# Reusing split weights at the start of the second token half, and data-paced constant matmuls, in a hybrid conv block

## Chip, cores and metric

The kernel runs on one core of a Trainium2 chip. The metric is the device time of one execution in microseconds, the median over runs. The profile is one separate execution, with its own time and span; all positions below are microseconds from the start of that span.

## The reference

One layer of a streaming encoder on 1024 tokens of 1024 channels (float32):

```python
h = rms_norm(x, norm_mix_g) * (1 + sc1) + sh1          # sh1, sc1, g1, ... = silu(c) @ w_ada + b_ada
proj = h @ w_in                                        # 1024 -> 7 x 1024
b_s, c_s, v_s, v_c, gl_c, gate_br = split(proj)
y_a = (b_s * causal_dwconv(c_s * v_s, conv_short_w)) @ w_short_out
u = v_c * sigmoid(gl_c)
u = causal_dwconv(u, conv_conf_w) + conv_conf_b        # width 31
y_b = silu(layer_norm(u)) @ w_conf_out
g_a, g_b = split(sigmoid(gate_br))
x = x + g1 * ((g_a * y_a + g_b * y_b) @ w_o)
h2 = rms_norm(x, norm_ffn_g) * (1 + sc2) + sh2
a, b = split(h2 @ w_ffn_in)
x = x + g2 * ((silu(a) * b) @ w_ffn_out)
out = rms_norm(x, final_norm_g)
```

## The kernel before

Activations lie transposed: 128 channels on the partitions, tokens along the row. [...] A matrix of weights comes in eight row chunks (128 input channels each) or column chunks.

For precision each float32 operand is split into a high part and a remainder: `split_w` (L208) has ScalarE (ACT) cast the loaded chunk `raw` to `wh` (L214) and VectorE (DVE) or GpSimd (POOL) subtract it to get `wl` (L215). The pools for `wh` and `wl` hold three chunks each, those for `raw` five in all. `mm3` (L301) then makes three matmuls per product: wh x high (L309), wh x remainder (L310), wl x high (L312). The first three chunks of the first stage, `WHOLE`, are multiplied unsplit in float32 (L305).

A list `plan` holds the order in which weights are loaded and split. `next_w(ahead)` takes the next ready chunk and first has `fetch` prepare `ahead` more; `AHEAD` is 2. The SP queue issues the loads in the order in which buffers come free. Each engine works its instructions in an order fixed when the program is built; a scheduler that models times chooses it, within the data dependencies and explicit `issue_after` hints.

The stages that the change touches:

- **Beginning** (L479 to L507). `c` is broadcast over the partitions by two matmuls into `cb` (L497). ACT squares the eight 512-token chunks of x into `sq` tiles (six-buffer pool `gs`), DVE adds them (`squares_x`, L428), two matmuls with a matrix of ones sum over channels into `ss` (`norm_start`, L440). ACT takes the reciprocal root into `rx0r` (L359) and squares it (L372); DVE refines it, writing `rx0r` in place (`rstd_negative`, L377 and L378); `modulate` scales x (DVE L388, ACT L392). `keep_clock` (L471) puts constant 128 x 128 matmuls of ones between: 7 before `cb`, 16 between `cb` and `ss`, 18 after `ss` (`CLOCK`).
- **Lead** (L554 to L560). Seven column blocks of the input projection by `row_blocks` (L408): for each row chunk k, all seven blocks, each in a PSUM bank of its own; then the same for the second half, with its own norm (`rx1`). `row_blocks` interleaves the last `joined` chunks block by block, so that banks finish one after the other. For the second half all eight chunks are loaded and split again (`again_w`).
- **yb** (L851 to L866). The Conformer branch's projection by `row_blocks` with eight blocks (all eight banks), first for one half, then the other. After a half each bank is multiplied with a gate tile `gb` on DVE (L860), which frees it; `join` adds `ma` (L848) and splits the sum into `mg` (ACT L340, DVE L341). The gate tiles come by DMAs that POOL issues (L859), six buffers for all. During the stage `next_b` also loads rows of `ada` into `raw` buffers, and DVE makes modulation values of them (L290).
- **Mix** (L872 to L887, L938 to L945). The output projection w_o, one column chunk after the other, first half then second half.

In yb and mix the plan loads all eight chunks of `w_conf` and `w_o` for each half. Every half takes the chunks in the order 0 to 7.

Of the kernel before, what the change touches and what calls it, by code (L numbers as in the profile page):

```python
# [65 lines left out]
WHOLE = 3  # L66


CLOCK = (7, 16, 18)


SQ_LAST = 2
# [43 lines left out]
def block_kernel(ctx: ExitStack, tc: tile.TileContext, x0, xT, c, vecs, ada, w_first, w_plain, w_duals,  # L116
# [32 lines left out]
    def ps2_tile(name):  # L149
        return ps2p.tile([P, H], F32, tag="ps2", name=name)  # L150
# [54 lines left out]
    def weights(src, n=1024, after=(), lo_engine=nc.vector):  # L205
        return split_w(load(src, n), n, after, lo_engine)
# [57 lines left out]
        units = dual_units([w_duals[d, m] for m in range(4)], 1024, eng=nc.gpsimd)  # L264
        plan += [units[m] for m in PRODUCTS]
    plan += [(w_short[k], 1024, (), nc.gpsimd) for k in range(KC)]
    plan += [(w[k], 1024) for w in (w_conf, w_o) for _ in range(2) for k in range(KC)]
    ready = []

    def next_w(ahead=AHEAD):  # L270

        fetch(ahead + 1)
        return ready.pop(0)
# [64 lines left out]
    def split(src, tile_of, name):  # L338
        hi, lo = tile_of(name + "h", dt=F32R), tile_of(name + "l", dt=F32R)
        nc.scalar.copy(hi, src)  # L340
        split.ins = nc.vector.tensor_tensor(lo, src, f32(hi), ALU.subtract).ins  # L341
        return hi, lo
# [26 lines left out]
    def rstd_square(begun):  # L369

        ss, eps, r, q, _ = begun
        nc.scalar.activation(q, r, AF.Square, scale=0.5 ** 0.5)  # L372
        return ss, r, q
# [12 lines left out]
    def modulate(src, r, scale, shift, name, begun=None):  # L386
# [14 lines left out]
        modulate.ins = begin.ins, act.ins, last.ins  # L401
        return hi, lo

    def first_operands(act, n=2):

        return [(next_w(), act(k)) for k in range(n)]

    def row_blocks(act, n, name, ops=(), unit=lambda k: next_w(), joined=2):  # L408


        outs = [(ps_tile if o < 6 else ps2_tile)(f"{name}{o}") for o in range(n)]
        ops = list(ops)
        for k in range(KC):
            if k == len(ops):
                xs = act(k)
                ops.append((unit(k), xs))
            if KC - joined <= k < KC - 1:
                continue
            for o in range(n):
                for kk in range(KC - joined, KC) if k == KC - 1 else (k,):  # L420
                    w, xs = ops[kk]
                    mm3([outs[o]], slice(o * P, o * P + P), w, [xs], kk == 0, kk == KC - 1)
        return outs
# [1 line left out]

    x = {}

    def squares_x(src, acc=None):  # L428

        for t in src:  # L430
            sq = g_tile("sq")
            act = nc.scalar.activation(sq, t, AF.Square, scale=1.0 / 32.0)
            if acc is None:
                acc = sq
            else:
                add = nc.vector.tensor_tensor(acc, acc, sq, ALU.add)
        squares_x.ins = act.ins, add.ins
        return acc

# [28 lines left out]
        nc.scalar.activation(sig, ps, AF.Sigmoid)  # L468
        nc.scalar.dma_start(gate_dram[b, j][:, halves[h]], sig)

    def keep_clock(ins, n):  # L471

        t = ps2_tile("clock")[:, :P]
        for _ in range(n):
            with tc.issue_after(ins) if ins else ExitStack():
                ins = nc.tensor.matmul(t, ones, ones, start=True, stop=True).ins
        keep_clock.ins = ins

    hT = [[None, None] for _ in range(KC)]  # L479
# [14 lines left out]
    for s in halves:  # L494
        cb.append(ps_tile("cb"))
        with tc.issue_after(keep_clock.ins):
            mm = nc.tensor.matmul(cb[-1], ones[:1], crow[:, s], start=True, stop=True)  # L497
    keep_clock(mm.ins, CLOCK[1])
    acc = squares_x([xin[k] for k in range(KC - SQ_LAST)])
    acc = [acc, squares_x([xin[k] for k in range(KC - SQ_LAST, KC)])]  # L500
    with tc.issue_after(squares_x.ins[0]):
        for s, t in zip(halves, cb):
# [1 line left out]
    with tc.issue_after(keep_clock.ins):  # L504
        rx_0 = norm_start(acc, "rx0")
    keep_clock(norm_start.ins, CLOCK[2])
    rx_0 = rstd_square(rx_0)  # L507

    def lead_w(k):
        if k < WHOLE:  # L510
            return load(w_first[k], LEAD * P), None
        return weights(w_first[k], LEAD * P, modulate.ins[:1])

    def act_x(k, h):
        nonlocal rx_0, rx_1
        if h == 0:
            with ExitStack() as after:
                after.enter_context(tc.issue_after(modulate.ins[0] if k else squares_x.ins[1]))
                for i in range(2 * k, 2 * k + 2):
                    modulation(i, ucp.tile([P, T + CK - 1], F32, tag="uc", name="ada")[:, :D])  # L520
            affine(naff1, k, 8, ng, V_GMIX)
            if k == 0:
                rx_0 = rstd_negative(*rx_0)
            x[k, 0] = s_tile(f"x{k}0")
        whole = h == 0 and k < WHOLE
        hT[k][h] = modulate(x[k, h], rx_1 if h else rx_0, naff1[:, k : k + 1], modc(k),
                            None if whole else f"h{k}{h}", None if h else xin[k])
        if h == 0:
            if k == X1_AT:
                for i in range(KC):  # L530
                    x[i, 1] = s_tile(f"x{i}1")
                    nc.sync.dma_start(x[i, 1], xT[i, :, halves[1]])
            elif k == X1_AT + 1:
                with tc.issue_after(modulate.ins[2]):
                    rx_1 = squares_x([x[i, 1] for i in range(KC)])
                with tc.issue_after(mm3.ins), tc.issue_after(modulate.ins[1]):
                    rx_1 = rstd_square(norm_start(rx_1, "rx1", ss_tile=ps2_tile))
            elif k == KC - 1:
                with tc.issue_after(modulate.ins[2]):
                    rx_1 = rstd_negative(*rx_1)  # L540
            if whole:
                return x[k, 0]
        elif 2 <= k < 2 + WHOLE:
            hT[k - 2][0] = split(x[k - 2, 0], hl_tile, f"h{k - 2}0")
        return hT[k][h]

    def again_w(k):

        return next_w(0 if k < KC - 2 else AHEAD)

    rx_1 = None
    plan[:KC] = [lambda k=k: weights(w_first[k], LEAD * P, [modulate.ins[0]]) for k in range(KC)]
    ops = ()
    for h in range(2):  # L554
        lead = row_blocks(lambda k: act_x(k, h), LEAD, "lead", ops, again_w if h else lead_w, 1 + h)
        if h == 0:
            ops = [(again_w(k), xs) for k, xs in ((k, act_x(k, 1)) for k in range(2))]
        for j in range(LEAD // 2):
            glu(j, h, lead[2 * j], lead[2 * j + 1])
        gate("b", 0, h, lead[-1])  # L560
# [234 lines left out]
    def act_b(k, h):  # L795
        z = cv[k][:, halves[h]]
        with ExitStack() as order:
            if (KC - 1, 1) in ma:
                order.enter_context(tc.issue_after(ma["ins"]))
            nc.vector.tensor_tensor(z, z, rl[h], ALU.mult)  # L800
        nc.scalar.activation(z, z, AF.Silu, bias=col(V_LNB, k), scale=col(V_LNG, k))
        zs[k, h] = split(z, s_tile, "zs")

    def next_b(k, h):

        if (k, h) < (KC - 1, 1):
            act_b(*((k + 1, h) if k < KC - 1 else (0, 1)))
        i = 24 + KC * h + k
        loaded.append((i, load(ada[i])))
        if len(loaded) > 1:  # L810
            with tc.issue_after(split.ins):
                modulation_of(*loaded.pop(0))
        return zs[k, h]


    for j in range(KC):
# [33 lines left out]

    ops = ()  # L851
    for h in range(2):
        yb = row_blocks(lambda k: next_b(k, h), KC, "yb", ops)
        if h == 0:
            ops = first_operands(lambda k: next_b(k, 1))
        gs = []
        for o in range(KC):
            g = g_tile("gb")
            nc.gpsimd.dma_start(g, gate_dram["b", o][:, halves[h]])  # L859
            nc.vector.tensor_tensor(g, yb[o], g, ALU.mult)  # L860
            gs.append(g)
            if o >= 4:
                join(o - 4, h, gs[o - 4])
        for o in range(KC - 4, KC):
            join(o, h, gs[o])
# [3 lines left out]
    x1 = [None] * KC  # L869
    x1_dram = [dram.tile([P, T], F32, name=f"x1_dram{j}") for j in range(KC)]  # L870

    def mix(j, h):  # L872
        xr = g_tile("xr")
        nc.gpsimd.dma_start(xr, xT[j, :, halves[h]])
        (o,) = col_block(next_w(), mg, (h,), "mix")
        if h == 0:
            x1[j] = ucp.tile([P, T + CK - 1], F32, tag="uc", name=f"x1{j}")[:, :T]
        dst = x1[j][:, halves[h]]
        nc.vector.scalar_tensor_tensor(out=dst, in0=o, scalar=modc(16 + j), in1=xr, op0=ALU.mult, op1=ALU.add)
        nc.gpsimd.dma_start(x1_dram[j][:, halves[h]], dst)  # L880
        sq = nc.scalar.activation(xr, dst, AF.Square, scale=1.0 / 32.0)
        if j == KC - 1:
            load_rsqrt(sq.ins)
        if j == 0:
            sums[h] = xr
        else:
            nc.vector.tensor_tensor(sums[h], sums[h], xr, ALU.add)  # L887
# [49 lines left out]

    sums = {}  # L938
    for h in range(2):
        for j in range(KC):  # L940
            mix(j, h)
            if h == 1 and j == 0:
                for k in range(KC):
                    affine(aff2, k, 32, vec, V_GFFN)
                norm_2_first()  # L945
# [355 lines left out]
```

## Time and profile before

| | |
|---|---|
| median of 3 runs | 1491.02 us (1489.75 to 1492.7) |
| profiled execution | 1494.91 us, its span 1493.1 us |
| PE busy | 1476.5 us, 99% |
| DVE busy | 1207.1 us, 81% |
| ACT busy | 597.6 us, 40% |
| POOL busy | 560.7 us, 38% |
| DMA | 247.79 MB, 166 GB/s over the span |

PE is TensorE's matmuls. A row of a timeline gives start, duration, engine, source line, operation, output<-input, and in brackets the idle time before it with what ended it. A row of the waits view gives total, times and longest wait. A row of the windows view gives the stretch and its length, then per engine the busy time and the count, then the granted clock and DMA figures. PE's matmuls overlap in the records: a row's duration is longer than the distance to the next start, and the distances are the pace.

### The profile page before, as it was taken

Reading aid. Unit: us, or ns where it says so; the run is one execution under the profiler, and the core shown is the slowest. Engines: PE = TensorE matmul, PEld = TensorE weight load, DVE = VectorE, ACT = ScalarE, POOL = GpSimd, SP = SyncE. Lnnn points to the kernel's source line nnn. Section 1 sums busy time; section 2 is a strip of 40 time slices with the busy share of each in tenths; the row PEclk is TensorE's granted clock in tenths of the full one; section 3 lists DMA queues with packets and bytes.
Section 4 is the critical chain, followed back from the end, with each engine's and each line's share of the span. In section 5 each row is a group of like instructions: output and inputs, shape, how many; then the busy total and the mean of one; then the engine's idle time right before and its main releaser. Section 6 shows DMA issues by size and latency. Waiting matters only on the chain.

```text
span 1493.1 us, 17891 instructions
## 1 busy us (share of the span) xinstructions
PE 1476.5 (99%) x6539; PEld 1211.6 (81%) x6539; DVE 1207.1 (81%) x1582; ACT 597.6 (40%) x854; POOL 560.7 (38%) x467
## 2 busy tenths in 40 slices
PE   9999999999999999999999999999999999999997
PEld 6788877888888887888788887888888888888887
DVE  6898899999899999758876699777777765677755
ACT  4753333333333344235335375444435443222235
POOL 0037768788788774410121001010111016545005
PEclk9999999999999999999999999999999999999999
DMA  8522213222223258456764425555555449998403
GB/s 332 215 78 71 99 57 128 71 85 99 85 71 99 59 210 317 147 184 225 254 205 159 159 87 195 185 183 180 176 177 171 152 152 371 351 310 261 137 29 113
DMA packets 83994, 247.79 MB, mean 166 GB/s; under 512 B 9665, under 2 KB 11841, under 8 KB 83906
## 3 DMA queue, kind: packets, MB, share of 16 engines
q1 hardware_dynamic: 43072, 138.43, 27.8%
q0 software_dynamic: 36944, 95.44, 19.4%
q10 hardware_dynamic: 3890, 12.78, 2.2%
q8 instruction: 51, 0.84, 0.2%
q14 instruction: 37, 0.30, 0.1%
HBM read 184.22 MB, written 62.39 MB: 165 GB/s over the span
## 4 chain that ended last, share of the span: by engine, by line
PE 47%; DVE 3%; issue 1%; POOL 0%; ACT 0%; DMA 0%; POOLq 0%; DVEq 0%; ACTq 0%
PE x L312 7%; PE x L309 7%; PE x L310 7%; PE z L312 4%; PE z L309 4%; PE z L310 4%; PE y L312 3%; PE y L310 3%; PE y L309 3%; PE mix L309 2%; PE mix L310 2%; PE mix L312 2%; PE yb L309 1%; PE yb L312 1%; PE yb L310 1%
## 5 line engine op out<-in xcount | busy, mean ns | idle before, releaser
L214 ACT CAST wh<-raw 128x1024 fp32r<-128x1024 f32 (+2 forms) x257 | 259.1, 1009 | 465.0 <-PE x L310 117.3
L215 POOL TENSOR_TENSOR wl<-raw,wh 128x1024 fp32r<-128x1024 f32 x92 | 238.8, 2602 | 114.2 <-ACT wh L214 105.7
L215 DVE TENSOR_TENSOR wl<-raw,wh 128x1024 fp32r<-128x1024 f32 (+2 forms) x165 | 188.2, 1141 | 43.5 <-ACT wh L214 41.2
L720 DVE SCALAR_TENSOR_TENSOR c<-diff,vec,c 128x512 f32<-128x512 f32 x232 | 172.2, 750 | 4.0
L1017 POOL DMA_DIRECT2D hid<-stage x71 | 37.8, 533 | 346.2 <-DVE stage L349 340.2
L309 PE MATMUL x<-th,wh 128*128 128x512 f32 x336 | 131.1, 390 | 2.4 <-DVE sig L602 1.3
L312 PE MATMUL x<-th,wl 128*128 128x512 f32 x336 | 130.7, 389 | 0.0
L310 PE MATMUL x<-tl,wh 128*128 128x512 f32 x336 | 130.7, 389 | 0.0
L720 DVE SCALAR_TENSOR_TENSOR c<-u,wsum,c 128x512 f32<-128x512 f32 x112 | 84.0, 750 | 2.1
L309 PEld LDWEIGHTS x<-th,wh 128*128 128x128 f32 x336 | 63.1, 188 | 16.8 <-DVE sig L602 1.7
L312 PEld LDWEIGHTS x<-th,wl 128*128 128x128 f32 x336 | 63.1, 188 | 13.0
L310 PEld LDWEIGHTS x<-tl,wh 128*128 128x128 f32 x336 | 63.1, 188 | 13.0
L309 PE MATMUL x<-t2h,wh 128*128 128x512 f32 x184 | 71.7, 390 | 1.6 <-ACT wh L214 1.2
L310 PE MATMUL x<-t2l,wh 128*128 128x512 f32 x184 | 71.5, 389 | 0.0
L312 PE MATMUL x<-t2h,wl 128*128 128x512 f32 x184 | 71.4, 390 | 0.1
L348 ACT CAST stage<-g 128x512 fp32r<-128x512 f32 x62 | 38.3, 621 | 79.8 <-DVE g L1006 39.8
L234 POOL TENSOR_TENSOR raw<-raw 128x1024 f32<-128x1024 f32 x12 | 29.7, 2478 | 96.8 <-DVE wl L215 94.8
L309 PE MATMUL z<-th,wh 128*128 128x512 f32 x168 | 65.4, 389 | 0.0
L310 PE MATMUL z<-tl,wh 128*128 128x512 f32 x168 | 65.4, 389 | 0.0
L312 PE MATMUL z<-th,wl 128*128 128x512 f32 x168 | 65.4, 389 | 0.0
L349 DVE TENSOR_TENSOR stage<-g,stage 128x512 fp32r<-128x512 f32 x62 | 42.3, 688 | 27.2 <-ACT stage L348 27.2
L1043 POOL DMA_DIRECT2D th<-hid x71 | 38.1, 536 | 47.9 <-PE x L312 27.3
(836 smaller groups left out, 4097.3 us busy)
## 6 DMA issues: line engine op xcount, KB each, us to landing
hid<-stage POOLq DMA_DIRECT2D x71, 512.0 KB, 4.6
raw<-in_w_fi SPq DMA_DIRECT2D x51, 512.0 KB, 4.0
raw<-in_w_duals SPq DMA_DIRECT2D x48, 512.0 KB, 3.5
th<-hid POOLq DMA_DIRECT2D x71, 256.0 KB, 5.7
tl<-hid POOLq DMA_DIRECT2D x71, 256.0 KB, 5.7
ada<-in_ada SPq DMA_DIRECT2D x24, 512.0 KB, 6.3
raw<-in_ada SPq DMA_DIRECT2D x24, 512.0 KB, 4.4
raw<-in_w_fo SPq DMA_DIRECT2D x24, 384.0 KB, 5.8
```

What stands on the lines that cost most here:

```text
L214: hi = nc.scalar.copy(wh, raw)
L215: lo = lo_engine.tensor_tensor(wl, raw, f32(wh), ALU.subtract)
L234: eng.tensor_tensor(a["s1"], a["21"], a["22"], ALU.add)
L309: nc.tensor.matmul(ps, wh, xh, start=first, stop=False, skip_group_check=again)
L310: nc.tensor.matmul(ps, wh, xl, start=False, stop=False, skip_group_check=again)
L312: mm3.ins = nc.tensor.matmul(ps, wl, xh, start=False, stop=last, skip_group_check=again).ins
L348: t_split.act = nc.scalar.copy(hi, src).ins
L349: t_split.ins = nc.vector.tensor_tensor(lo, src, f32(hi), ALU.subtract).ins
L720: tap.ins = nc.vector.scalar_tensor_tensor(out=out, in0=src[:, s : s + H], scalar=wt, in1=acc, op0=ALU.mult, op1=ALU.add).ins
L1017: nc.gpsimd.dma_start(hid_dram[key], s)
L1043: nc.gpsimd.dma_start(t, hid_dram[key][:, s])
```

## The change

The second half of lead, yb and mix takes the row (or column) chunks in the order 5, 6, 7, 0, 1, 2, 3, 4. Chunks 5, 6 and 7 of the first half are still in the three `wh`/`wl` buffers, so the second half uses these and neither loads nor splits them again; the first half fetches nothing beyond chunk 7. The second half's act operands (`act_x`, `next_b`, `mix`) follow the same order, and the three whole chunks are split for later use at the steps of chunks 0, 1, 2.

At the beginning the 16 constant matmuls before `ss` become two after each of the first five additions, with the square just added as moving operand; the 18 after `ss` become 6 with ones and 10 with `rx0r` as moving operand.

```diff
-CLOCK = (7, 16, 18)
+CLOCK = (7, 2, 6, 10)
+KEPT = 3
+SECOND = [*range(KC - KEPT, KC), *range(KC - KEPT)]
...
-    plan += [(w[k], 1024) for w in (w_conf, w_o) for _ in range(2) for k in range(KC)]
+    plan += [(w[k], 1024) for w in (w_conf, w_o) for ks in (range(KC), SECOND[KEPT:]) for k in ks]
...
+    kept = []
+
+    def first_w(k):
+        w = next_w(min(AHEAD, KC - 1 - k))
+        if k >= KC - KEPT:
+            kept.append(w)
+        return w
+
+    def second_w(i):
+        if i < KEPT:
+            fetch(i)
+            return kept.pop(0)
+        return next_w()
...
                 add = nc.vector.tensor_tensor(acc, acc, sq, ALU.add)
+                if clock:
+                    keep_clock(keep_clock.ins, clock, sq)
...
-    def keep_clock(ins, n):
+    def keep_clock(ins, n, src=None):
         t = ps2_tile("clock")[:, :P]
+        src = ones if src is None else src[:, :P]
         for _ in range(n):
             with tc.issue_after(ins) if ins else ExitStack():
-                ins = nc.tensor.matmul(t, ones, ones, start=True, stop=True).ins
+                ins = nc.tensor.matmul(t, ones, src, start=True, stop=True).ins
...
-    keep_clock(mm.ins, CLOCK[1])
-    acc = squares_x([xin[k] for k in range(KC - SQ_LAST)])
+    keep_clock.ins = mm.ins
+    acc = squares_x([xin[k] for k in range(KC - SQ_LAST)], clock=CLOCK[1])
...
     keep_clock(norm_start.ins, CLOCK[2])
+    keep_clock(keep_clock.ins, CLOCK[3], rx_0[2])
     rx_0 = rstd_square(rx_0)
...
-        elif 2 <= k < 2 + WHOLE:
-            hT[k - 2][0] = split(x[k - 2, 0], hl_tile, f"h{k - 2}0")
+        elif k < WHOLE:
+            hT[k][0] = split(x[k, 0], hl_tile, f"h{k}0")
...
-    def again_w(k):
-        return next_w(0 if k < KC - 2 else AHEAD)
+    def again_w(i):
+        if i < KEPT:
+            fetch(i // 2)
+            return kept.pop(0)
+        return next_w(1 if i < KC - 2 else AHEAD)
...
-        lead = row_blocks(lambda k: act_x(k, h), LEAD, "lead", ops, again_w if h else lead_w, 1 + h)
+        lead = row_blocks(lambda i: act_x(SECOND[i] if h else i, h), LEAD, "lead", ops, again_w if h else lead_w, 1 + h)
...
-        yb = row_blocks(lambda k: next_b(k, h), KC, "yb", ops)
+        yb = row_blocks(lambda i: next_b(KC * h + i), KC, "yb", ops, second_w if h else first_w)
...
-    def mix(j, h):
+    def mix(i, h):
+        j = SECOND[i] if h else i
...
-        (o,) = col_block(next_w(), mg, (h,), "mix")
+        (o,) = col_block((second_w if h else first_w)(i), mg, (h,), "mix")
```

More of the change, by code (lines that the diff above doesn't have):

```diff
@@ L402, in modulate, with row_blocks @@
         return hi, lo
+    kept = []
[9 more added lines that the diff above has]
+        return next_w()
     def first_operands(act, n=2):
-        return [(next_w(), act(k)) for k in range(n)]
-    def row_blocks(act, n, name, ops=(), unit=lambda k: next_w(), joined=2):
+        return [(second_w(i), act(i)) for i in range(n)]
+    def row_blocks(act, n, name, ops, unit, joined=2):
         outs = [(ps_tile if o < 6 else ps2_tile)(f"{name}{o}") for o in range(n)]
@@ L426, in block_kernel, with squares_x @@
     x = {}
-    def squares_x(src, acc=None):
+    def squares_x(src, acc=None, clock=0):
         for t in src:
@@ L511, in lead_w @@
             return load(w_first[k], LEAD * P), None
-        return weights(w_first[k], LEAD * P, modulate.ins[:1])
+        w = weights(w_first[k], LEAD * P, modulate.ins[:1])
+        if k >= KC - KEPT:
+            kept.append(w)
+        return w
     def act_x(k, h):
@@ L542, in act_x @@
                 return x[k, 0]
-        elif 2 <= k < 2 + WHOLE:
-            hT[k - 2][0] = split(x[k - 2, 0], hl_tile, f"h{k - 2}0")
+        elif k < WHOLE:
+            hT[k][0] = split(x[k, 0], hl_tile, f"h{k}0")
         return hT[k][h]
-    def again_w(k):
-        return next_w(0 if k < KC - 2 else AHEAD)
+    def again_w(i):
[3 more added lines that the diff above has]
+        return next_w(1 if i < KC - 2 else AHEAD)
     rx_1 = None
-    plan[:KC] = [lambda k=k: weights(w_first[k], LEAD * P, [modulate.ins[0]]) for k in range(KC)]
+    plan[:KC] = [lambda k=k: weights(w_first[k], LEAD * P, [modulate.ins[0]]) for k in SECOND[KEPT:]]
     ops = ()
     for h in range(2):
-        lead = row_blocks(lambda k: act_x(k, h), LEAD, "lead", ops, again_w if h else lead_w, 1 + h)
+        lead = row_blocks(lambda i: act_x(SECOND[i] if h else i, h), LEAD, "lead", ops, again_w if h else lead_w, 1 + h)
         if h == 0:
-            ops = [(again_w(k), xs) for k, xs in ((k, act_x(k, 1)) for k in range(2))]
+            ops = [(again_w(i), xs) for i, xs in ((i, act_x(SECOND[i], 1)) for i in range(2))]
         for j in range(LEAD // 2):
@@ L802, in act_b, with next_b @@
         zs[k, h] = split(z, s_tile, "zs")
[L804 to L809, printed above, removed]
+    order_b = [(k, 0) for k in range(KC)] + [(k, 1) for k in SECOND]
+    def next_b(i):
+        if i + 1 < 2 * KC:
+            act_b(*order_b[i + 1])
+        loaded.append((24 + i, load(ada[24 + i])))
         if len(loaded) > 1:
@@ L812, in next_b @@
                 modulation_of(*loaded.pop(0))
-        return zs[k, h]
+        return zs[order_b[i]]
     for j in range(KC):
@@ L852, in block_kernel @@
     for h in range(2):
-        yb = row_blocks(lambda k: next_b(k, h), KC, "yb", ops)
+        yb = row_blocks(lambda i: next_b(KC * h + i), KC, "yb", ops, second_w if h else first_w)
         if h == 0:
-            ops = first_operands(lambda k: next_b(k, 1))
+            ops = first_operands(lambda i: next_b(KC + i))
         gs = []
@@ L881, in mix @@
         sq = nc.scalar.activation(xr, dst, AF.Square, scale=1.0 / 32.0)
-        if j == KC - 1:
+        if i == KC - 1:
             load_rsqrt(sq.ins)
-        if j == 0:
+        if i == 0:
             sums[h] = xr
@@ L939, in block_kernel @@
     for h in range(2):
-        for j in range(KC):
-            mix(j, h)
-            if h == 1 and j == 0:
+        for i in range(KC):
+            mix(i, h)
+            if h == 1 and i == 0:
                 for k in range(KC):
```

## The prediction

> **What bounds the kernel now.** I read the page's engine shares first, then the view of who waited for whom on PE, then the timelines of the three places that the change touches.
>
> ```profile
> span 1493.1 us, 17891 instructions
> PE 1476.5 (99%) x6539; PEld 1211.6 (81%) x6539; DVE 1207.1 (81%) x1582; ACT 597.6 (40%) x854; POOL 560.7 (38%) x467
> PE yb L309 <- DVE gb L860: 2.2, 2, 2.0
> PE x L309 <- DVE sig L602: 1.3, 1, 1.3
> PE x L309 <- ACT wh L214: 1.2, 1, 1.2
> PE x L309 <- ACT sig L642: 0.9, 1, 0.9
> PE lead L305 <- ACT x L392: 0.4, 1, 0.4
> 910.00:1000.00 90.00, 90.00 (x399) 74.52 (x398) 69.70 (x88) 39.74 (x59) 11.18 (x21) 1.00 0.59 197
> L214 ACT CAST wh<-raw 128x1024 fp32r<-128x1024 f32 (+2 forms) x257 | 259.1, 1009 | 465.0 <-PE x L310 117.3
> L215 DVE TENSOR_TENSOR wl<-raw,wh 128x1024 fp32r<-128x1024 f32 (+2 forms) x165 | 188.2, 1141 | 43.5 <-ACT wh L214 41.2
> ```
>
> PE is busy for 99% of the span, and its waits sum to some 8 us. An undisturbed stretch has 399 matmuls in 90 us, 0.226 us each. The change keeps all matmuls of the result, so it can win only where PE stands still or does what no result needs: the beginning, and the places where a second half follows a first. The removed work is nine chunks of weights, each a load, a cast on ACT (mean 1.0 us) and a subtraction on DVE (mean 1.1 us): 9 us of ACT and 10 us of DVE, engines that are 40% and 81% busy. By itself that is worth nothing; it counts where those engines are late for PE.
>
> **The beginning.**
>
> ```profile
> 4.35 3.78 PE L497 MATMUL cb<-diff,ones 1*128 1x512 f32 x4
> 8.06 6.47 PE L476 MATMUL clock<-ones 128*128 128x128 f32 x32
> 14.36 1.88 PE L444 MATMUL ss<-sq,ones 128*128 128x512 f32 x4
> 16.08 4.18 PE L476 MATMUL clock<-ones 128*128 128x128 f32 x36
> 20.68 18.29 PE L305 MATMUL lead<-x,raw 128*128 128x512 f32 x42 [0.41 <-ACT x L392]
> 8.00:13.60 5.60, 5.54 (x26) 1.00 1.03 419
> 16.08:20.27 4.19, 4.18 (x36) 1.00 0.68 275
> 6.81 4.48 DVE L436 TENSOR_TENSOR sq<-sq 128x512 f32<-128x512 f32 x6
> 16.28 0.69 ACT L359 ACTIVATE rx0r<-ss,eps 128x512 f32<-128x512 f32 x1 [5.36 <-PE ss L444]
> 17.00 0.63 ACT L372 ACTIVATE rx0t<-rx0r 128x512 f32<-128x512 f32 x1
> 18.39 0.69 DVE L378 SCALAR_TENSOR_TENSOR rx0r<-rx0t,rx0r 128x512 f32<-128x512 f32 x1
> 19.11 0.75 DVE L388 SCALAR_TENSOR_TENSOR x<-x,naff,rx0r 128x512 f32<-128x512 f32 x1
> 19.90 0.72 ACT L392 ACTIVATE x<-x,mod 128x512 f32<-128x512 f32 x1 [2.27 <-DVE x L388]
> ```
>
> Each constant matmul leaves two records. Up to 13.6 us they run at 5.60/26 = 0.215 us a record, later at 4.19/36 = 0.116: the pace doubles at 13.6 us, though the clock column reads 1.00 in both stretches. The squares' sums are ready at 6.81 + 4.48 = 11.3 us, but the ss matmuls start at 14.36, behind 32 records. The new kernel has 20 there, each pair waiting for a square; ACT makes those squares early, so the pairs run back to back: 8.06 + 20 x 0.215, and 0.1 for the first, is 12.5 us. The ss takes 16.08 - 14.36 = 1.72 us in four records at full pace; a record and a bit run at half pace until 13.6, so ss ends at 14.7 instead of 16.1: 1.35 us won. The last two squares now also wait for a constant pair that reads the buffer which they take over; by the pair times that moves the last sum to 11.5 us, still under 12.5.
>
> Then it is lost again. Ten of the 16 matmuls behind ss read rx0r, and L378 writes rx0r in place: in the built order of the changed kernel that DVE instruction waits for PE, in the old one for DVE alone. The 32 records last 32 x 0.112 = 3.6 us, to 18.3, and with the drain of the last L378 starts at 18.5, against 18.39. Behind it are queued on DVE the modulate step and all later modulations, on ACT the L392, and for them PE waits. From L378 to the first lead matmul it is 20.68 - 18.39 = 2.29 us as before, so lead starts at 20.8: 0.1 us later, with PE idle for some 2.3 us ahead of it, 0.41 now.
>
> Whether the pace survives that gap: at 712.17 (rows in the yb part) PE stood for 1.98 us, and the matmuls at 715.12 and after run at normal pace, so I cost the gap at nothing more; would the pace fall, lead would be slow for as long as the rise took here, 8.06 to 13.6, and lose half of these 5.5 us, 2.75. [...]
>
> **The lead's second half.**
>
> ```profile
> 55.59 0.68 DVE L436 TENSOR_TENSOR sq<-sq 128x512 f32<-128x512 f32 x1
> 57.89 1.02 PE L444 MATMUL ss<-sq,ones 128*128 128x512 f32 x2
> 63.32 0.39 PE L312 MATMUL lead<-h70h,wl 128*128 128x512 f32 x1
> 63.83 1.20 PE L309 MATMUL lead<-h01h,wh 128*128 128x512 f32 x4
> 66.47 0.39 PE L312 MATMUL lead<-h01h,wl 128*128 128x512 f32 x1
> 66.86 0.50 PE L309 MATMUL lead<-h11h,wh 128*128 128x512 f32 x1
> ```
>
> PE starts 0.51 us after the last matmul of the first half, and 0.39 after 66.47, where 0.226 is due; with the slow second matmul behind each (0.1) that is 0.65 us. In the built order ss stands seven matmuls earlier (56.3 us, just as the last sum is done at 55.59 + 0.68), and DVE has no weight subtraction between the two norms' scaling and h51l. Following the chain with the rows' durations, h51h is ready at 62.3 and h51l at 63.4, for a need at 63.55. I take 0.6 us won; ends: 0 and 0.65.
>
> The kept buffers add one wait: chunk 0's cast cannot start until PE has done the second half's chunk 5, 21 x 0.226 = 4.75 us in, and ACT's later casts queue behind it. PE needs chunk 0 after 14.2 us, and cast and subtraction take 2.1, so 7 us of cover remain; the closest case is chunk 4, whose buffer is freed one chunk (4.75 us) before the joint block of chunks 3 and 4: cover 2.6 us. In yb and mix, with 24 matmuls a chunk, it is more. I cost this at nothing.
>
> **The yb stage's second half.**
>
> ```profile
> 712.17 0.39 PE L312 MATMUL yb<-zsh,wl 128*128 128x512 f32 x1
> 714.54 0.50 PE L309 MATMUL yb<-zsh,wh 128*128 128x512 f32 x1 [1.98 <-DVE gb L860]
> 715.12 0.39 PE L312 MATMUL yb<-zsh,wl 128*128 128x512 f32 x1
> 715.74 0.50 PE L309 MATMUL yb<-zsh,wh 128*128 128x512 f32 x1 [0.24 <-DVE gb L860]
> 703.12 1.28 DVE L290 CUSTOM_DVE_ANT_0 raw<-raw,cs,vec 128x1024 f32<-128x1024 f32 x1 [1.28 <-DMA raw<-in_ada]
> 704.34 2.48 DVE L860 TENSOR_TENSOR gb<-yb,gb 128x512 f32<-128x512 f32 x4
> 708.53 0.68 DVE L341 TENSOR_TENSOR mg00l<-gb,mg00h 128x512 fp32r<-128x512 f32 x1
> 709.51 0.54 POOL L859 DMA_DIRECT2D gb<-gate_b  x1 [9.38 <-DVE mg00l L341]
> 711.54 2.35 DVE L215 TENSOR_TENSOR wl<-raw,wh 128x1024 fp32r<-128x1024 f32 x2
> 713.81 0.68 DVE L860 TENSOR_TENSOR gb<-yb,gb 128x512 f32<-128x512 f32 x1
> ```
>
> Here PE wants the eight PSUM banks back in order. The eviction of the seventh (713.81) is late for three reasons in a row: DVE stood before a modulation whose transfer was late (703.12), so evictions began at 704.34; so the first gb tile was free only after 708.53, and the load into it was issued at 709.51; and two subtractions of second-half weights (711.54, 2.35 us) stood ahead. PE loses 2.37 - 0.23 and 0.62 - 0.23 us, and 0.1 behind each: 2.7 us. In the new order no subtraction stands among the evictions, the mg00l stands fourth instead of after six evictions and sums, and the modulation ahead of them takes its buffer from chunk 6's weights, not chunk 7's, so its load is issued one chunk (5 us) earlier. With 0.6 us a step, evictions then start when the first bank is done (9.4 us before the half ends), the seventh tile's load is issued 6 us and landed 2 us before the half ends, and all banks are back in time. I take 2.7 us; ends: 0 and 2.7, nearer to 2.7, since two of the three causes are gone by the order alone.
>
> **Mix and the rest.** Mix has no PE wait to lose; its three subtractions were beside matmuls. The "x" waits (3.4 us) lie in stages whose order on PE and DVE is unchanged; they move with the rest. They hang on how DVE and POOL fall together:
>
> ```profile
> 198.09 2.81 DVE L672 TENSOR_TENSOR u<-u,sig 128x512 f32<-128x512 f32 x1
> ```
>
> Such an operation takes 0.68 us elsewhere (55.59), so I allow 1 us either way.
>
> **Sum.** +0.1 - 0.6 - 2.7 = -3.2 us. On the profiled execution (1494.91 us, span 1493.1) that is 1491.7; on the median of the three runs, 1491.02, it is **1487.8 us**. The profiled execution is 3.9 us above that median, so its waits may be larger than usual.
>
> **Rivals.**
> - *L378 does not wait for the constant matmuls in effect*: lead starts at 20.68 - 1.35 = 19.3; -1.4 - 0.6 - 2.7 gives 1486.3. The built order's wait on PE speaks against it.
> - *The yb wait is replaced*: another late modulation transfer (DVE waits for such transfers in this stage, 1.28 us above) holds the evictions again. Then +0.1 - 0.6 is left: 1490.5, no measurable change.
> - *The clock stays low (slower)*: the paced matmuls leave PE at half pace through ss and into lead. Then ss ends at 12.5 + 3.4 = 15.9, the 32 records at 15.9 + 32 x 0.215 = 22.8, lead starts at 25.2, 4.5 us late, and slow at first, 2.75 us more: +7.2 - 3.3 = +3.9, 1495.0. It decides if the pace has not doubled when ss ends. Against it: by the square's times above the paced stretch has no holes, and the pace outlived the gap at 712.17.
>
> **How the numbers follow.** A measurement of this kernel can tell about 0.2% (3.0 us, below 1488.0) from no change. The forecast gets 0.60, its own range 1486.3 to 1489.0 with the 1 us of the "x" waits and partial wins, two thirds below 1488.0: 0.41 faster, 0.19 same. The first rival 0.10 (faster), the second 0.17 (same), the third 0.08 (slower), and 0.05 for a wait that I have not seen (slower). Faster 0.51, same 0.36, slower 0.13. The range leaves out the slower cases and the edge of the fast ones: 1485.2 to 1491.2.
>
> **What would show it.** Right: first lead matmul at 20.5 to 21.2 us, ss ending near 14.7, L378 released by PE; no PE wait on gb at L892 (the eviction's new line); 248 casts at the weight split instead of 257. Wrong: lead at 19.3, or at 25 with slow records; a PE wait of over 1 us in yb; a new PE wait on a weight cast in a second half.

## The result and the profile after

The changed kernel takes 1501.47 us (median of 6 runs, 1500.23 to 1504.9) against 1491.07 us for the kernel before on the same chip: ratio 1.007, 95% interval 1.0058 to 1.0083. It is slower by 10 us where 3 us of gain were forecast, far above the forecast 1485.2 to 1491.2 us. The profiled execution took 1500.65 us, its span 1498.9.

Distances between the first matmuls of the stages, from the two traces, show where it went:

| from, to | before, us | after, us | difference |
|---|---|---|---|
| span's start, lead | 20.7 | 18.7 | -2.0 |
| lead, gb | 81.65 | 80.92 | -0.7 |
| gb, x | 10.88 | 10.88 | 0 |
| x, ya (the duals stage) | 460.29 | 472.25 | **+12.0** |
| ya, yb | 91.3 | 90.6 | -0.7 |
| yb, mix | 89.84 | 87.04 | -2.8 |
| mix, end | 738.5 | 738.5 | 0 |

The differences sum to the 5.8 us between the two spans; the medians lie further apart because before's profiled execution was 3.9 us above its median. In the stages that the change edits nothing was lost. The loss is in a stage of which it edits no line. First the windows view of that stage, whole, of before and then of after (columns: stretch, length, then busy time and count of PE, PEld, DVE, ACT and POOL, granted clock, DMA share, GB/s):

```profile
113.21:573.50 460.29, 457.86 (x2018) 378.15 (x2017) 437.66 (x547) 163.24 (x219) 354.54 (x147) 1.00 0.30 101
```

```profile
110.51:582.76 472.25, 463.52 (x2017) 381.34 (x2016) 437.12 (x549) 164.67 (x221) 355.12 (x147) 0.99 0.30 101
```

PE has the same matmuls (the counts differ by one record). It is idle for 8.7 us where it was idle for 2.4, and its busy time has grown by 5.7 us, at a lower mean clock: 6.3 + 5.7 = 12.0. The waits view of after (who waited for whom: total, times, longest) names the idle part; before had no PE wait on `wl`:

```profile
PE x L317 <- POOL wl L220: 6.2, 3, 2.6
PE y L317 <- POOL wl L220: 2.5, 2, 2.2
PE lead L310 <- ACT x L397: 2.3, 1, 2.3
PE x L314 <- ACT wh L219: 1.2, 1, 1.2
```

The other part is the clock. The windows view of after, PE alone, at two of these stalls (stretch, length, busy time and count, granted clock, DMA share, GB/s):

```profile
198.80:202.20 3.40, 1.40 (x6) 1.00 0.08 14
202.20:205.60 3.40, 3.40 (x10) 0.50 0.41 147
205.60:209.00 3.40, 3.40 (x16) 1.00 0.44 154
...
540.10:543.50 3.40, 0.76 (x4) 1.00 0.38 154
543.50:546.90 3.40, 3.40 (x9) 0.50 0.26 107
```

Behind three of the stalls (2.63, 2.21 and 2.64 us) the clock column stands at 0.50 for 3.41 us, from 202.18, 430.87 and 543.51 us on. In the rows PE has 9 or 10 matmuls there instead of 16. Half of such a stretch is about 1.7 us, 5.1 for the three: an estimate of what they cost, beside the 5.7 by which PE's busy time has grown.

**Why POOL is late.** In a dual, seven products are made of four blocks of weights (11, 12, 21, 22) and sums of them. POOL first makes s1 = 21 + 22 (L239), then 21 + 11, then subtracts for product after product in the order 1, 2, 6, 5, 7, 3, 4. POOL's waits for ACT's casts and for these loads in the stretch 112 us to the stage's end, before and then after:

```profile
POOL wl L215 <- ACT wh L214: 85.7, 32, 7.9
POOL raw L234 <- DMA raw<-in_w_duals: 1.3, 1, 1.3
```

```profile
POOL wl L220 <- ACT wh L219: 70.1, 28, 7.2
POOL raw L239 <- DMA raw<-in_w_duals: 37.2, 11, 3.9
```

In each of the eleven duals that follow the first, s1 now waits some 3.4 us for a load. The timelines of POOL and of SP's issues around one of them, before and then after:

```profile
248.61 2.41 POOL L215 TENSOR_TENSOR wl<-raw,wh 128x1024 fp32r<-128x1024 f32 x1
253.68 2.40 POOL L215 TENSOR_TENSOR wl<-raw,wh 128x1024 fp32r<-128x1024 f32 x1 [2.66 <-ACT wh L214]
256.16 2.42 POOL L234 TENSOR_TENSOR raw<-raw 128x1024 f32<-128x1024 f32 x1
251.04 0.33 SPq L200 DMA_DIRECT2D raw<-in_w_duals  x1
```

```profile
252.23 2.40 POOL L220 TENSOR_TENSOR wl<-raw,wh 128x1024 fp32r<-128x1024 f32 x1 [3.03 <-ACT wh L219]
258.18 2.40 POOL L239 TENSOR_TENSOR raw<-raw 128x1024 f32<-128x1024 f32 x1 [3.55 <-DMA raw<-in_w_duals]
254.66 0.33 SPq L205 DMA_DIRECT2D raw<-in_w_duals  x1
```

Before, the last of the next dual's four loads is issued at 251.04, when the subtraction of product 3 has ended, and has landed by 256.16. After, it is issued at 254.66, behind the subtraction of product 4, the dual's last, and s1 starts 3.5 us later, when it has landed. POOL stands, and its subtractions come later; shorter waits for ACT (70.1 us for 85.7) take up part of it, and five times a `wl` is too late for PE. The issue times show what each load waits for. Before, the four are issued at 238.36, 240.73, 245.24 and 251.04, each within 0.1 us of the end of a subtraction: those of products 6, 5, 7 and 3. After, it is 237.62, 243.80, 249.23 and 254.66, behind products 6, 7, 3 and 4.

The reason lies in a line that the diff does not show:

```python
raws = [rawp] * 3 + [rawbp] * 2

def raw_tile(n=1024):
    raws.append(raws.pop(0))
    return raws[-1].tile([P, 1024], F32, tag="raw", name="raw")[:, :n]
```

The five raw buffers are two pools, of three and of two, taken in a fixed turn, and a dual takes five tiles, 11, 12, 21, 22 and s1: one whole turn. So each block always meets the same pool, and which one depends on how many tiles were taken ahead of the first dual, modulo five. Before it was 8 + 8 + 1 = 17. The change drops three loads from lead's second half: 14. The buffers of a dual are given back in the order 11, s1, 21, 12, 22 (after products 6, 5, 7, 3, 4). With 17, 22 shares its pool with 11 and s1, and the built program has the new 22 in the old s1's buffer, free early (the issue behind product 5 above). With 14, 22 shares with 12 and 21, and the new 22 gets the old 22's buffer, free last (the issue behind product 4). That is the theory (below: the turn). Its rivals: the start's new pacing, the kept weights or new order as such, or POOL and DVE falling together otherwise.

### The profile page after: what moved, and what is told of

Its sections match the earlier page's. It is cut to its first block, busy times and chain, and to the rows that moved or that the text cites. A ratio compares the mean times of both kernels' runs of the same rounds, so it can differ in the third digit from the quotient of the medians.

```text
span 1498.9 us, 17818 instructions
## 1 busy us (share of the span) xinstructions
PE 1476.3 (98%) x6523; PEld 1212.1 (81%) x6523; DVE 1190.0 (79%) x1573; ACT 591.0 (39%) x845; POOL 557.6 (37%) x467
## 4 chain that ended last, share of the span: by engine, by line
PE 87%; DVE 5%; POOL 4%; issue 1%; DMA 1%; ACT 1%; POOLq 0%; ACTq 0%; DVEq 0%
PE x L317 11%; PE x L314 11%; PE x L315 11%; PE z L314 6%; PE z L315 6%; PE z L317 6%; PE y L317 4%; PE y L314 4%; PE y L315 4%; PE ya L314 2%; PE yb L317 2%; PE yb L314 2%; PE ya L315 2%; PE ya L317 2%; PE yb L315 2%; POOL wl L220 2%
## 5 line engine op out<-in xcount | busy, mean ns | idle before, releaser
L219 ACT CAST wh<-raw 128x1024 fp32r<-128x1024 f32 (+2 forms) x248 | 250.2, 1009 | 482.8 <-PE z L315 111.7
L220 POOL TENSOR_TENSOR wl<-raw,wh 128x1024 fp32r<-128x1024 f32 x92 | 237.3, 2587 | 95.4 <-ACT wh L219 91.3
L220 DVE TENSOR_TENSOR wl<-raw,wh 128x1024 fp32r<-128x1024 f32 (+2 forms) x156 | 177.6, 1139 | 36.5 <-ACT wh L219 35.1
L239 POOL TENSOR_TENSOR raw<-raw 128x1024 f32<-128x1024 f32 x12 | 29.5, 2455 | 128.6 <-DVE wl L220 91.4
L314 PEld LDWEIGHTS x<-th,wh 128*128 128x128 f32 x336 | 63.1, 188 | 13.6 <-DVE z L633 0.3
```

The source lines that it names most:

```text
L219: hi = nc.scalar.copy(wh, raw)
L220: lo = lo_engine.tensor_tensor(wl, raw, f32(wh), ALU.subtract)
L239: eng.tensor_tensor(a["s1"], a["21"], a["22"], ALU.add)
L314: nc.tensor.matmul(ps, wh, xh, start=first, stop=False, skip_group_check=again)
```

## The experiments

Each kernel was timed against the kernel before on the same chip, whose medians there were 1491.8 to 1493.0 us.

**1. The old turn in the new kernel (e1_turn3).** Three places of the turn are skipped when the first dual's first unit is made:

```diff
+    def turned(unit):
+        def first():
+            for _ in range(TURN):          # TURN = 3
+                raws.append(raws.pop(0))
+            return unit()
+        return first
...
+        if d == 0:
+            units["1"] = turned(units["1"])
```

> The changed kernel, with the turn of the five raw buffers moved on by three places just before the first dual's loads, so that the duals meet the buffers as they did in the kernel before (eleven loads, casts and subtractions after the turn, nothing else changed). Turn theory: the stage from the first x matmul to the first ya matmul goes back from 472.3 to about 460.5 us, POOL's L240 sum no longer waits 3.5 us a dual for a load (37 us in all now, 1 to 7 then), no PE wait on a wl cast of over 1 us; the time is 1501.5 - 12 = about 1489, between 1486 and 1490. If the start's new pacing or the kept weights themselves lengthen the duals: stays at 1500 to 1502.

Measured: 1489.58 us, ratio 0.9984 (0.9976 to 0.9993). The stage is 460.35 us and PE's waits on `wl` are gone. All of the loss was the turn.

**2. The new turn in the old kernel (e2_before_turn2).** The same edit in the kernel before, with `TURN = 2`.

> The kernel before, with the turn of the raw buffers moved on by two places just before the first dual, which gives the turn that the changed kernel has there; none of the change is in it. Turn theory: 11 waits of POOL's L235 sum for a load, some 35 to 40 us in all, duals stage about 472, time about 1491 + 12 = 1503 (1500 to 1505). If the cause is the start's pacing or the kept weights: 1490 to 1492, no change.

Measured: 1503.57 us, ratio 1.0071 (1.0056 to 1.0085), as large as the change's own loss. Its waits view shows the signature, with nothing of the change in it:

```profile
PE x L324 <- POOL wl L216: 6.2, 3, 2.6
PE y L324 <- POOL wl L216: 2.5, 2, 2.0
...
POOL raw L235 <- DMA raw<-in_w_duals: 36.9, 11, 3.8
```

**3 and 4. The change's halves (e3_order_only, e4_clock_only).** Order and kept weights alone (old `CLOCK`), and pacing alone (old order):

```diff
-CLOCK = (7, 2, 6, 10)
+CLOCK = (7, 16, 18)
-    keep_clock.ins = mm.ins
-    acc = squares_x([xin[k] for k in range(KC - SQ_LAST)], clock=CLOCK[1])
+    keep_clock(mm.ins, CLOCK[1])
+    acc = squares_x([xin[k] for k in range(KC - SQ_LAST)])
...
-    keep_clock(keep_clock.ins, CLOCK[3], rx_0[2])
```

> The changed kernel with the constant matmuls of the start as before: only the order of the second halves and the kept weights. Turn theory: three loads fewer ahead of the duals are still there, so duals stage about 472 and time 1500 to 1503; lead starts near 20.7 us. Start's pacing as the cause: duals stage 460, time about 1488.

> The kernel before with the new pacing of the constant matmuls alone; second halves in the old order. Turn theory: duals stage about 460, and the time is that of before, with lead starting between 18.7 and 20.8 us: 1489 to 1491.5. Start's pacing as the cause: duals stage 472, time 1500 to 1503.

Measured: order alone is at 1501.33 us, ratio 1.0054 (1.0035 to 1.0072), stage 472.2 us; pacing alone at 1492.01 us, ratio 1.0 (0.999 to 1.0009), stage 460.4 us. That median is 0.5 us above the expected 1489 to 1491.5, but no different from before's. The pacing has no part in the loss.

**5 and 6. Which turns are bad (e5_turn4, e6_turn2)?** As 1, with `TURN = 4` and `TURN = 2`, two turns that neither kernel has.

> As e1_turn3, but the turn is moved on by four places: another turn than the kernel before has (blocks 11 and 12 in raw_b, 21, 22 and the sum s1 in raw). Turn theory in its exact form (a dual is slow where the load of 22 can only take the buffer of the old 22, which is the last that a dual gives back): here 21 takes the buffer of s1 and 22 that of 21, both given back early, so the duals are as fast as in e1: stage 460 to 461 us, under 3 us of waits of L240 for loads, time 1488 to 1491. If only the turn of the kernel before is a good one: stage near 472, time near 1501.

> As e1_turn3, but the turn is moved on by two places (blocks 11, 12 and s1 in raw, 21 and 22 in raw_b). Exact form of the turn theory: 21 takes the buffer of 21 and 22 that of 22, given back last, though the turn is not the one of the changed kernel: L240 waits 11 times for a load, 35 to 40 us in all, stage 471 to 473 us, three windows at half clock or so, time 1500 to 1503. If only the changed kernel's own turn is bad: stage 460, time near 1489.5.

Measured: turn 4: 1489.16 us, ratio 0.9983 (0.9974 to 0.9991). Turn 2: 1503.8 us, ratio 1.0073 (1.0055 to 1.0091). The stages in the windows view, PE alone, first of turn 4 and then of turn 2:

```profile
110.91:570.03 459.12, 457.93 (x2017) 1.00 0.30 101
```

```profile
112.07:586.78 474.71, 464.81 (x2018) 0.99 0.30 100
```

So it is not that any turn but the old one is bad. Four of the five turns have now been run, two good and two bad, and what decides is whether 22 must wait for the old 22's buffer. Turn 4 is even 1.2 us shorter in the stage than turn 3: a PE wait on `sig` of 1.4 us is gone with it. Turn 2 exceeded the expected 471 to 473 us (and the expected time): one stall was followed by two stretches of 3.4 us at half clock (PE busy 464.81 us, for 463.52 in after), and PE's waits on `wl` sum to 9.8 us instead of 8.7.

**7 and 8. Another remedy (e11_22_first, e13_22_first_here).** No turn, but a dual takes its buffers in another order, so that with 14 tiles ahead 22 gets the pool that s1 has:

```diff
-                get("11", "12", "21", "22")
+                get("22", "11", "12", "21")
```

> The changed kernel with one line's order changed and no turn: each dual takes the buffers for its four blocks in the order 22, 11, 12, 21 and not 11, 12, 21, 22. With 14 buffers taken ahead of the duals, 22 and s1 then share the pool of two, so that 22 takes the buffer of the old s1, given back early. Turn theory (it is the late load of 22 that costs the time, not the number 14): stage 460 to 461 us, under 3 us of waits of POOL's sum for loads, time 1488.5 to 1490.5. If the removed loads ahead of the duals cost it in some other way: 1500 to 1502.

Measured: 1495.61 us, ratio 1.0023 (1.0014 to 1.0033): missed. The stage was cured, 460.4 us. But the line also serves the last stage, and mix to the end took 743.2 us instead of 738.5; the timelines show casts and sums there waiting for loads of `w_fo`, and PE behind them. The first row is PE's, the others ACT's and DVE's:

```profile
1291.87 0.50 PE L314 MATMUL x<-th,wh 128*128 128x512 f32 x1 [1.68 <-ACT wh L219]
1290.98 1.57 ACT L219 CAST wh<-raw 128x768 fp32r<-128x768 f32 x2 [13.28 <-DMA raw<-in_w_fo]
1290.91 0.96 DVE L241 TENSOR_TENSOR raw<-raw 128x768 f32<-128x768 f32 x1 [5.76 <-DMA raw<-in_w_fo]
```

The other 1.7 us of that trace are a drop of the clock at the start of lead (lead to gb 82.6 us, not 80.9; below). So the order was limited to the first stage's duals, by an argument of `dual_units`:

> e11_22_first was 1495.6, though its duals stage was back at 460.4 us; its line serves the last stage's duals (w_fo) too, and there stalls of 1.0, 2.1, 0.7 and 1.4 us appeared at 1280 to 1309 us, behind loads of w_fo. Here the order 22, 11, 12, 21 holds for the first stage's duals alone. Turn theory, with e11's miss put down to the last stage: stage 460 to 461 us, mix to the end 738 to 739 us as in e1 (743.2 in e11), time 1488.5 to 1490.5. If the miss has another cause: near 1495.

Measured: 1490.85 us, ratio 0.9991 (0.9979 to 1.0004); stage 460.1 us, mix to the end 738.5 us. The miss was the last stage's. The median lies a little above the expected range; its profiled execution had a late start (lead at 20.25 us, below).

**9 to 11. The wait of L383 (e7_turn3_ones, e12_22_first_ones, e10_turn4_ones).** The prediction had DVE's L383 wait for the ten constant matmuls which read the tile that it writes. In after's timeline of DVE it does:

```profile
14.23 0.69 DVE L382 SCALAR_TENSOR_TENSOR rx0t<-ss,rx0t 128x512 f32<-128x512 f32 x1 [0.54 <-ACT rx0t L377]
16.42 0.69 DVE L383 SCALAR_TENSOR_TENSOR rx0r<-rx0t,rx0r 128x512 f32<-128x512 f32 x1 [1.50 <-PE clock L500]
17.14 0.75 DVE L393 SCALAR_TENSOR_TENSOR x<-x,naff,rx0r 128x512 f32<-128x512 f32 x1
```

The edit that takes the wait away, on turn 3, on the order of experiment 7, and on turn 4:

```diff
-    keep_clock(keep_clock.ins, CLOCK[3], rx_0[2])
+    keep_clock(keep_clock.ins, CLOCK[3])
```

> e1_turn3, with the last ten constant matmuls reading the ones and not rx0r, so that the DVE instruction which writes rx0r in place no longer waits for them. If that wait costs what the prediction took for it: from the end of ss to the first lead matmul 4.6 us as in the kernel before, not 6.07; lead starts at 17.4 us, not 18.9; time 1489.6 - 1.4 = 1488.2 against e1. If the path to lead does not run through it: lead at 18.9 and 1489.6.

> e11_22_first, with the last ten constant matmuls reading the ones and not rx0r. In the traces this took 1.5 us off the way from the end of ss to lead (4.6 for 6.07 us) and the 2.3 us gap of PE ahead of lead, after which the clock fell in one execution out of six; the medians of e1 and e7 did not show it (1489.58 and 1489.65). Expected: lead at 17.1 to 17.5 us, 1487.5 to 1489.5; if the gain is given back later, as between e1 and e7, the same as e11.

> e5_turn4, with the last ten constant matmuls reading the ones and not rx0r: the second try of the same step. Expected: lead at 17.1 to 17.5 us, time 1489.16 - 1.5 = 1487.7 (1487 to 1489); if the gain is given back later, 1489.2.

Measured: 1489.65 us, ratio 0.9984 (0.9975 to 0.9993); 1493.9 us, 1.0012 (1.0003 to 1.0021); 1487.66 us, 0.9966 (0.9954 to 0.9978). In all three traces lead follows the end of ss (the next matmul's start) in 4.6 us instead of 6.06, and PE stands 0.9 us ahead of it instead of 2.3. Of the 1.5 us, 0.4 come back within lead (lead to gb 81.4 us, 80.9 to 81.0 with the wait). In the medians the step won 1.7 us on experiment 7 (same chip) and 1.5 on turn 4 (two chips; by the ratios to the kernel before 2.5), and nothing on turn 3, where the trace has 1.0 us more between mix and the end than experiment 1's. Of that, 0.8 us are a wait of PE on `g` that experiment 1's trace has not; why it appears, is open. So the expected times were met on turn 4 alone; on experiment 7 its loss in the last stage remained. Turn 4 with this edit is the best kernel found, faster than before and than the change.

**12. Kept weights without the lead (e9_yb_mix_only).** Only yb and mix take chunks 5 to 7 first; lead and pacing are as before, so 17 tiles are still taken ahead of the duals:

> The kernel before, with the kept weights and the new order in yb and mix alone: lead and the start are as before, so the same 17 buffers are taken ahead of the duals and nothing is turned. Turn theory: duals stage 460 us although weights are kept; yb stage 87.0 us as in the changed kernel, against 88.2 to 89.8 in the traces with the old order; time 1.2 to 2.8 us below the kernel before. If kept weights as such cost something in the stages: no gain or above the kernel before.

Measured: 1491.43 us, ratio 0.9986 (0.9977 to 0.9996); stage 460.3 us, yb to mix 87.04 us. The gain is 1.0 us by the medians and 2.1 by the ratio. Kept weights harm nothing where they leave the turn alone.

## Why the prediction was wrong

**The step that failed** stands under "Mix and the rest": that the waits in the duals stage "lie in stages whose order on PE and DVE is unchanged; they move with the rest", with 1 us either way. The order was unchanged indeed on PE and ACT, and on DVE and POOL but for one pair of neighbours each. What changed was which buffer each load waits for, and with it the order and time of SP's issues. The first part had costed the removed loads as ACT and DVE time alone; that each also took one place of a turn did not appear. The 0.05 kept for an unseen wait was for this. The term measured +12.0 us.

**The rest, term by term.**

- *Start, +0.1 forecast.* ss ended near 12.65 us, not 14.7, and lead began at 18.7, not 20.8. Yet the mechanism held: L383 is released by PE, 1.50 us late, and lead follows the end of ss by 6.06 us, for the 6.1 worked out. What was mis-sized is the time at which the clock rises, which differs between executions. The timelines of PE in two more kernels, first the old pacing (experiment 12), then the new (experiment 8), show each with the other's rise:

```profile
4.35 1.98 PE L518 MATMUL cb<-diff,ones 1*128 1x512 f32 x4
6.26 5.46 PE L497 MATMUL clock<-ones 128*128 128x128 f32 x32
11.56 1.88 PE L465 MATMUL ss<-sq,ones 128*128 128x512 f32 x4
17.87 3.70 PE L310 MATMUL lead<-x,raw 128*128 128x512 f32 x8 [0.41 <-ACT x L397]
```

```profile
4.35 3.78 PE L521 MATMUL cb<-diff,ones 1*128 1x512 f32 x4
12.48 1.88 PE L467 MATMUL ss<-sq,ones 128*128 128x512 f32 x4
20.25 1.13 PE L310 MATMUL lead<-x,raw 128*128 128x512 f32 x2 [2.33 <-ACT x L397]
```

  With the late rise (12.5 to 13.6 us; cb takes 3.78) lead begins at 20.3 to 20.7 with the old pacing and 20.25 with the new; there ss starts at 12.48, for 12.5 forecast. With the early rise (near 4 to 5 us; cb takes 1.98 to 2.3) it is 17.87 with the old and 18.5 to 19.1 with the new. So the term was -0.2 or about +0.9 (from one trace each of the old pacing with the early rise and the new with the late one), and the -2.0 between the two traces belongs to the execution, not to the change. Ten of the traces have the early rise and four the late one; what decides between the two, no run shows.
- *The gap ahead of lead, at nothing.* So it was in after, but not always. Of seven traces with that gap of 2.3 us, two lost time to it (lead to gb 82.6 us, not 80.9), and stalls of 2.63, 2.21 and 2.64 us in after's duals did the same. Such a loss is about 1.7 us, half of one stretch of 3.41 us at half clock, not the 2.75 that the prediction named.
- *Lead's second half, -0.6 forecast.* -0.7 in after. It comes from both halves of the change: the new order alone gives 81.41 us (experiment 3), the pacing alone 81.18 (experiment 4), for 81.65 before. So the order, for which 0.6 was forecast, gave some 0.25 (also 81.4 in experiments 9 to 11, where PE stands 0.9 us ahead of lead); the rest comes with the gap ahead of lead. That the sum came out near is luck.
- *yb's second half, -2.7 forecast.* -2.8 against the profiled execution, and no PE wait on gb at L892. But the old order took 88.2 us in experiments 2 and 4, so the gain over a usual execution is 1.2 us. The prediction had warned that this execution's waits may be larger than usual.
- *The rivals.* The rival in which L378 does not wait and the one of a replaced yb wait did not occur. Nor did that of a low clock: the pace had doubled when ss ended (12 records in 1.33 us in after, 0.111 us each, for 0.215 at half pace), though by an earlier rise than was forecast.
- *Removed casts, kept buffers, mix, at nothing.* Confirmed: the cast's row has 248, mix to the end is unchanged, and no second half waits for a cast.

```profile
L219 ACT CAST wh<-raw 128x1024 fp32r<-128x1024 f32 (+2 forms) x248 | 250.2, 1009 | 482.8 <-PE z L315 111.7
```

With the turn put right, the kernel is at 1489.58 us, within the forecast range, and its ratio 0.9984 has the forecast one (1487.8/1491.02 = 0.9978) inside its interval. The reasons for a gain were sound in direction, but the closeness is partly luck: with lead's -0.7, yb's -1.2 against a usual execution and the start's -0.2 to +0.9 the terms make -1.0 to -2.1, not -3.2. One shared counter, not costed, outweighed them with its 12 us.

## What to carry to other kernels

Where buffers are handed out in a turn, a removed or added allocation shifts every later user: count the allocations ahead of each later stage, modulo the turn, and look up which operation gives back the buffer that each load will take. "The order on the engines is unchanged" says nothing of that; compare the queue's issues and the buffers. A remedy in a shared line must be followed through every stage that calls it.

## What the runs showed of the hardware

- In after the clock column reads 0.50 in four stretches of 3.41 us, from 7.62, 202.18, 430.87 and 543.51 us on, and 1.00 between them. In the rows of after's stalls above, PE was busy for 1.40 and 0.76 of 3.40 us, and the next 3.40 us are at half clock. Around before's yb stall (1.98 us) and the gap ahead of lead in after (2.32 us) the clock did not drop; the first rows are before's, the others after's:

```profile
709.90:713.30 3.40, 2.66 (x12) 1.00 0.48 154
713.30:716.70 3.40, 1.92 (x7) 1.00 0.72 246
```

```profile
14.40:17.80 3.40, 1.98 (x18) 1.00 1.01 400
17.80:21.20 3.40, 2.50 (x6) 1.00 0.65 184
```

  Behind the same gap ahead of lead in experiment 6 (2.33 us) the clock did drop:

```profile
15.30:18.70 3.40, 1.07 (x10) 1.00 1.01 408
18.70:22.10 3.40, 3.40 (x5) 0.50 0.63 205
```

  Behind the same stall in the last stage (1.68 us in experiment 7) the clock dropped in experiment 10 (first two rows) and not in experiment 7 (last two):

```profile
1288.00:1291.40 3.40, 1.46 (x6) 1.00 1.25 401
1291.40:1294.80 3.40, 3.40 (x10) 0.50 0.26 83
```

```profile
1288.40:1291.80 3.40, 1.78 (x8) 1.00 1.21 392
1291.80:1295.20 3.40, 3.08 (x12) 1.00 0.89 283
```

  So in these traces a stall of 1.7 to 2.6 us cost about 1.7 us more, or nothing. What decides between the two, no run shows.
- The clock also dropped where PE had not stood. With the early rise in experiment 12 PE is busy through 3.41 us, and the clock column reads 0.50 in the next 3.42:

```profile
4.31:7.72 3.41, 3.41 (x18) 1.00 1.02 400
7.72:11.14 3.42, 3.42 (x19) 0.50 1.02 416
```

  1.98 us of the first row are the cb matmuls (1*128 in their row). In eight of the ten early traces the clock falls at this place; in after it is at half from 7.62 us, behind 3.41 us in which PE was busy for 2.95, and the 20 constant records ahead of ss take 4.02 us, for 2.79 in experiments 6 and 7, where it does not fall. Why, no run shows.
- Before's times lie in two groups some 3 us apart (on one chip 1489.0 to 1490.3 and 1493.4 to 1496.7, with two between). With the old pacing the early and the late rise of the clock set lead 2.4 to 2.8 us apart (17.87 against 20.27 to 20.68), which would explain it. It is argued, not shown: only single executions have traces.
